# Gate matrix of an expert layer: one-hot matmuls replaced by indirect DMAs that add into HBM

## The chip, the core and the metric

The kernel runs on one core of a Trainium2 chip. The core has four compute engines that run side by side and meet through semaphores: TensorE (PE; its weight loads, PEld, are listed apart), VectorE (DVE), ScalarE (ACT) and GpSimd (POOL). SyncE (SP) here only issues DMAs. Sixteen DMA engines move data between HBM and the on-chip memory. The metric is device time of one execution in microseconds (us); less is better.

## The reference, cut to what matters

Two transformer blocks run one after the other over 256 tokens of width 1024. The first has a mixer (window attention and retention) and a gated FFN. The second has another mixer and, as its FFN, a layer of 16384 experts: each expert is one row of `expert_u` and one row of `expert_v`. Eight heads pick 16 experts each for every token, and only those 128 count, each with a softmax gate `g`:

```python
q = (xb @ w_query).reshape(PEER_TOKEN_BLOCK, PEER_HEADS, 2, PEER_HALF)
sc = jnp.einsum('thpd,hpkd->thpk', q, sub_keys).astype(jnp.float32)
s_top, i_top = lax.top_k(sc, PEER_TOPK)
cand = s_top[:, :, 0, :, None] + s_top[:, :, 1, None, :]
cand_idx = i_top[:, :, 0, :, None] * PEER_NKEYS + i_top[:, :, 1, None, :]
...
best, pos = lax.top_k(cand, PEER_TOPK)
eidx = jnp.take_along_axis(cand_idx, pos, axis=-1)
g = jax.nn.softmax(best, axis=-1)
u = jnp.take(expert_u, eidx, axis=0)
h = jax.nn.gelu(jnp.einsum('thkd,td->thk', u, xb))
vv = jnp.take(expert_v, eidx, axis=0)
return jnp.einsum('thk,thkd->td', (g * h.astype(jnp.float32)).astype(xb.dtype), vv)
```

An expert has the number 128 a + b, with a and b the picks of the head's two halves.

## The kernel before, in words

The kernel does not gather experts. It computes all 16384 of them for all tokens, in two layers. The first layer (`first_layer(j)`, j from 0 to 127) makes u x for the 128 experts of block j (all a, b = j) and puts its gelu into the matrix S (128 experts a, 128 blocks, 256 tokens) in the on-chip memory. S is multiplied by a gate matrix of the same shape, zero wherever an expert was not picked, and the second layer (`second_layer`, j from 0 to 127) sums S times v.

Every product is made in three passes for precision: a weight unit of 512 KB is loaded into a tile `raw` by SP (L89), split into a rounded part `whi` by ACT (L94) and a rest `wlo` by DVE (L95), and PE does hi x hi, hi x lo and lo x hi (`mm3`, L107 to L109). One unit of the first layer is 24 matmuls over 256 tokens. There are 433 such splits on DVE from start to end, one per unit apart from six that POOL does near the start; the first layer's last unit is the 305th, the second layer's units are the 306th to the 433rd. Four `raw` tiles and, in the expert layers, three pairs of `whi` and `wlo` let loads and splits run ahead of PE. The tile scheduler that orders each engine's instructions gives these loads and splits a higher priority (`AHEAD`), so they stand earlier than the code has them.

The picks are made beside the first queries and the first third of the first layer. For each head `choose(hd)` takes the best 16 of both halves and of 80 candidate sums on DVE. A generator (`all_steps`) yields these steps, and `pump` issues a budget of them after each query (PQ) and each first-layer unit (PU). When all eight heads are chosen, `decode()` turns the positions into pairs (a, b) with one-hot compares on DVE, makes the softmax gates, and transposes a, b and g on PE (L796) into the rows `gs`.

The gate matrix is then made four tokens at a time by `combine(jd)`, 64 times, between first-layer units: DVE makes a one-hot matrix of a (A) and of b (B), ACT and DVE scale B by the two halves of the gate (G), and PE multiplies A by G for each token and half (L872, eight matmuls of 128 x 128 per call). DVE multiplies the result into the part of S that is there already (L875), ACT writes the rest (L878), and units that come later multiply their gelu by what stands there (L934). So the end of the first layer and the gate matrix are interleaved on PE. The first block's FFN (`w_gate` and `w_up`, 22 units each) is where the change adds stores.

Of the kernel before, what the change touches and what calls it, by code (L numbers as in the profile page):

```python
# [22 lines left out]
GP = 115  # L23
# [4 lines left out]
GSCALE = 32768.0  # L28
# [7 lines left out]
for _n, _w in (("norm_mix", 8), ("norm_ffn", 8), ("final_norm", 8), ("ln_mix", 8), ("ln_ffn", 8),  # L36
               ("ret_gain", 8), ("gmlp_gain", 4), ("q_g", 1), ("k_g", 1), ("sinks", 8)):
    SMALL[_n] = (_o, _o + _w)
    _o += _w
# [3 lines left out]
class Net:  # L43
# [70 lines left out]
    def gemm_t(self, ps, src, hl, K, k0=0, first=True, last=True, parts=None, engine=None):  # L114
        """ps[n, t] += W[k, n] x[k, t] for one unit of up to 8 k."""
# [12 lines left out]
    def gemm_t_late(self, jobs, hl):  # L128
        """gemm_t of several (ps, src), with the last k after all others."""
# [6 lines left out]
    def gemm_n(self, src, hl):  # L136
        """two banks, one per 128 tokens, of [t, 512] for a chunk of 512 columns."""
# [19 lines left out]
    def rsqrt(self, y, ss, n, scale, pool=None):  # L157
        """y = (ss * scale + eps)^-1/2, all [128, n]."""
# [22 lines left out]
    def token_sums(self, acc):  # L181
        """[128 t, 2] from [128 d, 256 t] summed over d."""
# [6 lines left out]
    def rows(self, r, name):  # L189
        """[128, 256] with r of token t in column t, in every partition."""  # L190
# [40 lines left out]
    def block1(self, actp):  # L231
        nc, a, tc = self.nc, self.a, self.tc
        mult, add, sub = OP.mult, OP.add, OP.subtract
        with ExitStack():
# [125 lines left out]
            with ExitStack() as s1:  # L360
                p = self.pool("ffn", 1, s1)
                p2 = self.pool("ffn2", 2, s1)
                hid = self.new_acts(p, KF, "hid", 1)
                early = []
                for f in range(KF):
# [11 lines left out]
                    early.append((ps.rearrange("p (a t) -> p a t", a=2), None))  # L377
                    if f == 1:
                        continue
# [322 lines left out]
    def peer(self, st, x3, h, acc):  # L702
        nc, a, tc = self.nc, self.a, self.tc
        mult, add, sub = OP.mult, OP.add, OP.subtract
        with tc.using_default_side("right"):
            xb = self.new_acts(self.pool("xb", 1), tag="xb", bufs=1)
            gs = self.pool("gs", 1).tile([128, 4, T], F16, name="gs")
            qp = self.pool("query", 1)
            late = ExitStack()
            p = self.pool("topk", 1, late)  # L710
        hand = self.pool("hand", 2, st)
# [3 lines left out]
        best = p.tile([128, 8, 2, 16], F32, name="best")  # L715
        pos = p.tile([128, 8, 2, 16], U32, name="pos")
# [28 lines left out]
        def decode():  # L745
            e16 = p.tile([128, 2, 16, 8], F16, tag="cand", name="e16", bufs=2)
            t8 = p.tile([128, 8, 2, 16], U32, tag="sc", name="t8", bufs=SC)
            dec = p.tile([128, 4, 2, 16, 8], F16, tag="stop", name="dec")
            a16, b16 = dec[:, 0], dec[:, 1]

            def spot(x):
                return x.rearrange("p t k h -> p h t k")

            for e in range(2):
                yield 340, lambda: nc.vector.tensor_copy(spot(dec[:, 2 + e]), itop[:, :, :, e])
            yield 340, lambda: nc.vector.tensor_scalar(t8, pos, 56, None, op0=add)
            yield 340, lambda: nc.vector.tensor_scalar(spot(e16), pos, 72.0, 0.0, op0=sub, op1=OP.max)
            yield 340, lambda: nc.vector.tensor_scalar(t8, t8, 3, None, op0=OP.logical_shift_right)
            yield 340, lambda: nc.vector.tensor_scalar(spot(a16), t8, 8.0, 0.0, op0=sub, op1=OP.max)
            yield 340, lambda: nc.vector.tensor_scalar(t8, pos, 16.0, 8.0, op0=OP.is_lt, op1=mult)  # L760
            yield 340, lambda: nc.vector.scalar_tensor_tensor(spot(b16), spot(a16), -8.0, pos, op0=mult, op1=add)
            yield 340, lambda: nc.vector.scalar_tensor_tensor(spot(b16), t8, -8.0, spot(b16), op0=add, op1=add)
            yield 200, lambda: nc.vector.tensor_tensor(out=a16, in0=a16, in1=e16, op=add)
            yield 200, lambda: nc.vector.tensor_tensor(out=b16, in0=b16, in1=e16, op=sub)
            ex = p.tile([128, 8, 2, 16], F32, tag="itop", name="ex")
# [320 lines left out]
```

## Time and profile before

| | |
|---|---|
| three timed runs | 1341.98, 1343.14, 1346.91 us; median 1343.14 |
| profiled execution, first to last instruction (span) | 1343.6 us |
| TensorE busy | 1334.3 us, 99% |
| VectorE busy | 935.0 us, 70% |
| ScalarE busy | 768.4 us, 57% |
| GpSimd busy | 9.7 us, 1% |
| HBM read and written | 232.62 and 2.10 MB |

The profiled execution lies within the spread of the timed runs; beside its span the profile lists no other time of its own. Busy time is the share of the span in which an engine had an instruction under way; PE's instructions overlap one another, so that a matmul's own duration is longer than the step from one to the next. The chain of waits follows the work that ended last backwards, and says which engine's time makes up the span. Groups are named by source line, engine, operation and `out<-in`; buffer numbers are left out.

### The profile page before, as it was taken

Reading aid. Unit: us, or ns where it says so; the run is one execution under the profiler, and the core shown is the slowest. Engines: PE = TensorE matmul, PEld = TensorE weight load, DVE = VectorE, ACT = ScalarE, POOL = GpSimd, SP = SyncE. Lnnn points to the kernel's source line nnn. Section 1 sums busy time; section 2 is a strip of 40 time slices with the busy share of each in tenths; the row PEclk is TensorE's granted clock in tenths of the full one; section 3 lists DMA queues with packets and bytes.
Section 4 is the critical chain, followed back from the end, with each engine's and each line's share of the span. In section 5 each row is a group of like instructions: output and inputs, shape, how many; then the busy total and the mean of one; then the engine's idle time right before and its main releaser. Section 6 shows DMA issues by size and latency. Waiting matters only on the chain.

```text
span 1343.6 us, 24086 instructions
## 1 busy us (share of the span) xinstructions
PE 1334.3 (99%) x9384; PEld 1245.0 (93%) x9384; DVE 935.0 (70%) x1826; ACT 768.4 (57%) x1306; POOL 9.7 (1%) x12
## 2 busy tenths in 40 slices
PE   8999999999999999999999999999999999999998
PEld 8878999999998899999999999999998888888887
DVE  6767576766666977966996667777656666665665
ACT  5456445544455766444458887776555555555553
POOL 2000000000000000000000000000000000000000
PEclk8999999999999999999999999999999999999999
DMA  8545666666566446656564444444576666666664
GB/s 267 179 137 159 187 179 185 186 189 181 176 192 228 142 138 181 191 180 184 151 197 147 142 141 137 140 137 139 157 219 190 192 198 191 194 195 191 196 194 126
DMA packets 67633, 236.27 MB, mean 176 GB/s; under 512 B 7616, under 2 KB 9536, under 8 KB 67392
## 3 DMA queue, kind: packets, MB, share of 16 engines
q1 hardware_dynamic: 66512, 233.14, 57.1%
q8 instruction: 73, 1.20, 0.4%
q10 hardware_dynamic: 1008, 1.61, 0.3%
q14 instruction: 40, 0.33, 0.1%
HBM read 232.62 MB, written 2.10 MB: 175 GB/s over the span
## 4 chain that ended last, share of the span: by engine, by line
PE 95%; DVE 2%; DMA 1%; issue 0%; ACT 0%; POOL 0%; SPq 0%; ACTq 0%; POOLq 0%; DVEq 0%
PE ax L974 26%; PE mm L107 21%; PE mm L109 21%; PE mm L108 21%; PE ax L872 5%; DVE wlo L95 1%; DMA raw<-in_w_in_a_dram 1%; PE ax L837 0%; DMA xT<-in_xT_dram 0%; ACT whi L94 0%; PE ax L663 0%; PE ax L698 0%; PE ax L464 0%; PE ax L452 0%; PE ax L685 0%
## 5 line engine op out<-in xcount | busy, mean ns | idle before, releaser
L95 DVE TENSOR_TENSOR wlo<-raw,whi 128x1024 fp32r<-128x1024 f32 (+2 forms) x433 | 524.5, 1213 | 225.9 <-ACT whi L94 224.8
L94 ACT ACTIVATE whi<-raw 128x1024 fp32r<-128x1024 f32 (+3 forms) x439 | 458.0, 1046 | 332.9 <-PE mm L108 249.0
L107 PE MATMUL mm<-xbh,whi 128*128 128x256 f32 x1104 | 316.2, 287 | 0.0
L109 PE MATMUL mm<-xbh,wlo 128*128 128x256 f32 x1104 | 312.4, 283 | 0.8 <-DVE wlo L95 0.7
L108 PE MATMUL mm<-xbl,whi 128*128 128x256 f32 x1104 | 312.1, 283 | 0.0
L107 PE MATMUL mm<-acth,whi 128*128 128x256 f32 x848 | 241.0, 284 | 1.7 <-ACT acth L248 1.0
L108 PE MATMUL mm<-actl,whi 128*128 128x256 f32 x848 | 239.7, 283 | 0.7 <-DVE actl L249 0.7
L109 PE MATMUL mm<-acth,wlo 128*128 128x256 f32 x848 | 239.6, 283 | 0.0
L109 PEld LDWEIGHTS mm<-xbh,wlo 128*128 128x128 f32 x1104 | 210.6, 191 | 1.3 <-DVE wlo L95 1.2
L107 PEld LDWEIGHTS mm<-xbh,whi 128*128 128x128 f32 x1104 | 211.2, 191 | 0.2
L108 PEld LDWEIGHTS mm<-xbl,whi 128*128 128x128 f32 x1104 | 210.8, 191 | 0.0
L107 PEld LDWEIGHTS mm<-acth,whi 128*128 128x128 f32 x848 | 161.3, 190 | 2.8 <-ACT acth L248 1.2
L108 PEld LDWEIGHTS mm<-actl,whi 128*128 128x128 f32 x848 | 161.2, 190 | 1.6 <-DVE actl L249 1.6
L109 PEld LDWEIGHTS mm<-acth,wlo 128*128 128x128 f32 x848 | 161.3, 190 | 0.2 <-DVE wlo L95 0.2
L974 PE MATMUL ax<-wlo,keys 128*128 128x512 f32 x512 | 158.0, 389 | 0.0
L974 PE MATMUL ax<-whi,q 128*128 128x512 f32 x512 | 158.0, 389 | 0.0
L974 PE MATMUL ax<-whi,keys 128*128 128x512 f32 x512 | 157.9, 389 | 0.0
L151 ACT ACTIVATE keys<-S 128x256 fp32r<-128x256 f32 x128 | 53.4, 418 | 151.5 <-PE ax L974 151.5
L974 PEld LDWEIGHTS ax<-whi,q 128*128 128x128 f32 x512 | 96.1, 188 | 20.0
L974 PEld LDWEIGHTS ax<-wlo,keys 128*128 128x128 f32 x512 | 96.1, 188 | 19.9
L974 PEld LDWEIGHTS ax<-whi,keys 128*128 128x128 f32 x512 | 96.1, 188 | 19.8
L865 ACT ACTIVATE G<-B,ga 128x128 f16<-128x128 f16 x256 | 98.0, 575 | 0.0
(277 smaller groups left out, 1468.7 us busy)
## 6 DMA issues: line engine op xcount, KB each, us to landing
raw<-in_peer_u_dram SPq DMA_DIRECT2D x128, 512.0 KB, 3.6
raw<-in_peer_v_dram SPq DMA_DIRECT2D x128, 512.0 KB, 4.2
raw<-in_w_in_b_dram SPq DMA_DIRECT2D x32, 512.0 KB, 4.3
raw<-in_w_in_a_dram SPq DMA_DIRECT2D x31, 512.0 KB, 3.9
raw<-in_w_gate_dram SPq DMA_DIRECT2D x22, 512.0 KB, 3.6
raw<-in_w_up_dram SPq DMA_DIRECT2D x22, 512.0 KB, 3.7
raw<-in_w_out_dram SPq DMA_DIRECT2D x16, 512.0 KB, 4.3
raw<-in_w_down_dram SPq DMA_DIRECT2D x16, 512.0 KB, 3.6
```

The lines of the kernel that those rows point to most:

```text
L94: self.last_copy = nc.scalar.activation(hi[:, s], raw[:, s], AF.Copy).ins
L95: (engine or nc.vector).tensor_tensor(out=lo[:, s], in0=raw[:, s], in1=hi[:, s].bitcast(F32), op=OP.subtract)
L107: mm(ps, lhsT=left[0], rhs=right[0], start=first, stop=False)
L108: mm(ps, lhsT=left[0], rhs=right[1], start=False, stop=False)
L109: mm(ps, lhsT=left[1], rhs=right[0], start=False, stop=last)
L151: nc.scalar.activation(hi, src, AF.Copy)
L865: nc.scalar.activation(G[0][:, :, t], B[:, :, t], AF.Copy, scale=ga[:, t0 + t:t0 + t + 1])
L872: nc.tensor.matmul(C[:, t * 128:t * 128 + 128], lhsT=A[:, :, t], rhs=G[i][:, :, t], start=i == 0, stop=i == 1)
L974: nc.tensor.matmul(banks[tb][d], lhsT=s[left][:, ts], rhs=w[right][:, d * 512:d * 512 + 512], start=first, stop=end)
```

## The change

The one-hot matmuls, `combine` and the transposes are gone. Two matrices `cmat` are made in HBM, one for each half of the tokens, each 8 MB: element (a, b, t). They are zeroed by 32 stores of 512 KB that SP issues in the first block's FFN (L382). `decode` now runs four times, after every second head, for those two heads, and instead of a transposed list it makes for each pick the place 16384 a + 128 b + t in `pos` and the gate in `best`. Then `put` issues 64 indirect DMAs on POOL's queue: each takes one pick of one head for 128 tokens, and adds 128 gates of 4 bytes to 128 computed places (L809). All DMAs into one matrix are ordered by waits, each for the one before it; the two matrices are independent, which makes two chains of 128.

`gates(j)` loads four blocks j of the gate matrix from both `cmat` into a tile C (two DMAs of 256 KB on POOL's queue, three such tiles) and multiplies S by it on DVE (L937), 32 times in all. `first_layer` now always writes its whole gelu into S.

```diff
-        def combine(jd):
-            ...
-            nc.vector.tensor_tensor(out=B, in0=self.iota16, in1=spread(3), op=OP.is_equal)
-            for i in range(2):
-                if i == 0:
-                    for t in range(4):
-                        nc.scalar.activation(G[0][:, :, t], B[:, :, t], AF.Copy, scale=ga[:, t0 + t:t0 + t + 1])
-                else:
-                    nc.vector.tensor_tensor(out=G[i], in0=B, in1=spread(i), op=mult)
-            nc.vector.tensor_tensor(out=A, in0=self.iota16, in1=spread(2), op=OP.is_equal)
-            C = self.ax_bank()
-            for t in range(4):
-                for i in range(2):
-                    nc.tensor.matmul(C[:, t * 128:t * 128 + 128], lhsT=A[:, :, t], rhs=G[i][:, :, t], start=i == 0,
-                                     stop=i == 1)
-            ...
-            elif j % 2:
-                while done < T and done * (GP - start) < T * (j - start):
-                    combine(j + 1)
-        while done < T:
-            combine(128)
...
+                zero = p.tile([128, 1024], F32, name="zero")
+                nc.gpsimd.memset(zero, 0.0)
+                self.cmat = [tc.dram_tile([128 * 128 * 128, 1], F32, name=f"cmat{i}") for i in range(2)]
+                blank = [c.rearrange("(p n) o -> p (n o)", p=128) for c in self.cmat]
...
+                    for i in range(2 * f - 10, 2 * f - 8) if f >= 5 else ():
+                        if i < 32:
+                            nc.sync.dma_start(out=blank[i // 16][:, i % 16 * 1024:i % 16 * 1024 + 1024], in_=zero)
...
-        def decode():
+        def decode(h0):
...
+            for e, x in ((1, b16), (0, a16)):
+                ...
+                if e:
+                    place = p.tile([128, 64], F32, name="place")
+                    yield 130, lambda: nc.vector.scalar_tensor_tensor(
+                        place, oh[:, 0], 128.0, self.col("part").to_broadcast([128, 64]), op0=mult, op1=add)
+                else:
+                    yield 130, lambda: nc.vector.scalar_tensor_tensor(
+                        ps, spot(oh[:, 0].rearrange("p (k q) -> p k q", q=4)), 16384.0,
+                        spot(place.rearrange("p (k q) -> p k q", q=4)), op0=mult, op1=add)
...
+            def put():
+                for hd in range(2):
+                    for k in range(16):
+                        for tb in range(2):
+                            nc.gpsimd.indirect_dma_start(
+                                cmat[tb], bass.IndirectOffsetOnAxis(ap=ps[:, hd, tb, k:k + 1], axis=0),
+                                bs[:, hd, tb, k:k + 1], None, compute_op=add)
+
+            yield 10, put
...
                 yield from choose(hd)
-            yield from decode()
+                if hd % 2:
+                    yield from decode(hd - 1)
...
+            nc.scalar.activation(S[:, j - 1:j + 1], pair.rearrange("p (e t) -> p e t", e=2), AF.Gelu_apprx_tanh)
...
+        def gates(j):
+            C = cp.tile([128, 2, 4, 128], F32, name="C", bufs=3)
+            for tb in range(2):
+                nc.gpsimd.dma_start(out=C[:, tb], in_=cview[tb][:, j:j + 4])
+            Sj = S[:, j:j + 4].rearrange("p j (b t) -> p b j t", b=2)
+            nc.vector.tensor_tensor(out=Sj, in0=Sj, in1=C, op=mult)
+
+        gates(0)
+        gates(4)
...
-            if j == 32:
+            if j % 4 == 0 and j < 120:
+                gates(j + 8)
+            if j == 120:
                 groups.close()
```

The last `if` stands in the loop of the second layer; what follows it is the load of `x3`, the residual, which came at j = 32 and now comes at j = 120.

Where instructions moved, first POOL's queue. Before, POOL had nothing to do behind the two fills of the second block's mixer (L530, L532):

```order
L530 MEMSET rel_4859 64x8x64 [waits DMAHW4_49,DMAHW6_49,DVE_49,PE_49]
L532 MEMSET wsT_4862 64x8x64 [waits DMAHW5_49,Pool_49]
L1082 UNCONDITIONAL_BRANCH
```

Now the indirect DMAs follow there, the two matrices by turns. `DMASW` names the semaphore of a DMA that POOL issued: a row waits for the one two rows ahead of it.

```order
L537 MEMSET wsT_4900 64x8x64 [waits DMAHW5_49]
L809 DMA cmat0_2480<-best_5918,pos_5919 2097152x1 [waits DVE_49,PE_49,Activation_49]
L809 DMA cmat1_2481<-best_5918,pos_5919 2097152x1
L809 DMA cmat0_2480<-best_5918,pos_5919 2097152x1 [waits DMASW0_49]
L809 DMA cmat1_2481<-best_5918,pos_5919 2097152x1 [waits DMASW1_49]
L809 DMA cmat0_2480<-best_5918,pos_5919 2097152x1 [waits DMASW2_49]
L809 DMA cmat1_2481<-best_5918,pos_5919 2097152x1 [waits DMASW3_49]
```

There are 256 such rows, and behind the last of them on the same queue the 64 gate loads. The rows that wait for DVE as well are the first of each batch of 64; on DVE, the rows that release them (the write of `pos`, L796, or of `best`, L802) stand behind the 183rd, 199th, 213th and 219th wlo.

The second place is DVE at the 290th wlo, 15 units before the end of the first layer. Before, between two weight splits stood the making of one-hot tiles and the multiplies into S:

```order
L95 TENSOR_TENSOR wlo_11868<-raw_11866,whi_11867 128x1024 [waits DMAHW7_49,Activation_49]
L934 TENSOR_TENSOR S_6217<-S_6217,gt_11708 128x2x228 [waits Activation_49]
L875 SCALAR_TENSOR_TENSOR S_6217<-ax_11723,S_6217 128x110x4 [waits Activation_49]
L875 SCALAR_TENSOR_TENSOR S_6217<-ax_11745,S_6217 128x110x4 [waits PE_49]
L867 TENSOR_TENSOR G1_11846<-B_11844,gs_5868 128x512 [waits DVE_49]
L868 TENSOR_TENSOR A_11843<-iota16_139,gs_5868 128x512
L861 TENSOR_TENSOR B_11931<-iota16_139,gs_5868 128x512 [waits DVE_49,Activation_49]
L95 TENSOR_TENSOR wlo_11898<-raw_11896,whi_11897 128x1024 [waits DMAHW0_49,PE_49,Activation_49]
```

Now the first gate multiplies (L937) stand there, with the weight splits (L93 in the new numbering) between them; L150 are splits of S for the second layer:

```order
L93 TENSOR_TENSOR wlo_10782<-raw_10780,whi_10781 128x1024 [waits DMAHW7_49,PE_49,Activation_49]
L937 TENSOR_TENSOR S_6252<-S_6252,C_11275 128x2x4x128 [waits DMASW1_49,DMASW0_49]
L93 TENSOR_TENSOR wlo_10812<-raw_10810,whi_10811 128x1024 [waits DMAHW0_49,PE_49,Activation_49]
L937 TENSOR_TENSOR S_6252<-S_6252,C_11279 128x2x4x128 [waits DMASW3_49,DMASW2_49]
L150 TENSOR_TENSOR q_11294<-S_6252,keys_11293 128x256 [waits Activation_49]
L937 TENSOR_TENSOR S_6252<-S_6252,C_11309 128x2x4x128 [waits DMASW5_49,DMASW4_49]
L93 TENSOR_TENSOR wlo_10844<-raw_10842,whi_10843 128x1024 [waits DMAHW1_49,PE_49,Activation_49]
```

All 32 gate multiplies come within the next 21 weight splits, the last behind the 311th.

The third place is SP in the first block's FFN. Before, only weight loads stand there, gate and up by turns. Now the stores of zeros stand among them, some with a wait of their own:

```order
L87 DMA raw_2664<-in_w_up_dram 128x1024 [waits DMAHW2_49,DMAHW1_49,DVE_49]
L382 DMA cmat0_2480<-zero_2476 128x1024
L87 DMA raw_2714<-in_w_gate_dram 128x1024 [waits DMAHW5_49,DMAHW3_49,DVE_49]
L382 DMA cmat0_2480<-zero_2476 128x1024 [waits DMAHW4_49]
L87 DMA raw_2744<-in_w_up_dram 128x1024 [waits DMAHW7_49,DVE_49]
L87 DMA raw_2781<-in_w_gate_dram 128x1024 [waits DMAHW6_49,DMAHW0_49,DVE_49]
```

A load behind such a store is issued only after it; 32 stores stand among 37 loads.

## Rows read from the trace of the kernel before

**Rows 1.** Page, part 1: busy us, share of the span, instructions of each engine.
```profile
PE 1334.3 (99%) x9384; PEld 1245.0 (93%) x9384; DVE 935.0 (70%) x1826; ACT 768.4 (57%) x1306; POOL 9.7 (1%) x12
```

**Rows 2.** Page, part 4: the chain that ended last, by line.
```profile
PE ax L974 26%; PE mm L107 21%; PE mm L109 21%; PE mm L108 21%; PE ax L872 5%; DVE wlo L95 1%; DMA raw<-in_w_in_a_dram 1%; PE ax L837 0%; DMA xT<-in_xT_dram 0%; ACT whi L94 0%; PE ax L663 0%; PE ax L698 0%; PE ax L464 0%; PE ax L452 0%; PE ax L685 0%
```

**Rows 3.** Chain in order of time, from us 688: start, us, engine, tile, line.
```profile
688.41 0.33 PE ax L796 x3
...
712.10 1.89 PE ax L872 x16
...
955.94 0.96 PE ax L872 x8
991.45 347.52 PE ax L974 x1533
1339.00 1.37 DVE x L997 x2
```

**Rows 4.** Line L872: duration in ns (least, median, most), starts, forms.
```profile
L872 PE MATMUL ax<-G,A x512: 283/297/304, 711.9 to 956.6; 128*128 128x128 f16 x171
```

**Rows 5.** wlo on DVE from the start: stretch, length, busy (count), PEclk.
```profile
0.00:568.30 568.30, 218.72 (x183) 0.99 0.59 182
0.00:616.20 616.20, 238.25 (x199) 0.99 0.59 182
0.00:679.50 679.50, 262.56 (x219) 0.99 0.59 181
0.00:935.00 935.00, 348.36 (x290) 1.00 0.56 171
```

**Rows 6.** PE alone in the last combines and the second layer, same columns.
```profile
936.00:991.30 55.30, 55.30 (x464) 1.00 0.55 162
1000.00:1330.00 330.00, 330.00 (x1458) 1.00 0.64 192
```

**Rows 7.** DMA issues: out<-in, queue, count, KB each, median us to landing.
```profile
raw<-in_peer_v_dram SPq DMA_DIRECT2D x128, 512.0 KB, 4.2
...
out_dram<-x SPq DMA_DIRECT2D x2, 256.0 KB, 2.1
```

**Rows 8.** Page, part 5: line L95 (busy, mean ns, idle before).
```profile
L95 DVE TENSOR_TENSOR wlo<-raw,whi 128x1024 fp32r<-128x1024 f32 (+2 forms) x433 | 524.5, 1213 | 225.9 <-ACT whi L94 224.8
```

**Rows 9.** Page, part 3: all DMA queues: packets, MB, share.
```profile
q1 hardware_dynamic: 66512, 233.14, 57.1%
q8 instruction: 73, 1.20, 0.4%
q10 hardware_dynamic: 1008, 1.61, 0.3%
q14 instruction: 40, 0.33, 0.1%
```

**Rows 10.** Line L919, stores of x3t: issue ns, and us to landing.
```profile
L919 ACTq DMA_DIRECT2D x3t<-xt x4: 326/328/347, 511.7 to 516.8; - x4
...
DMA to landing us min/median/max: 2.4/3.3/6.4
```

**Rows 11.** Line L896, the loads of keys, the same.
```profile
L896 SPq DMA_DIRECT2D keys<-in_keys_dram x8: 328/342/424, 501.7 to 610.3; - x8
...
DMA to landing us min/median/max: 2.2/3.5/6.7
```

**Rows 12.** All engines in the first FFN: busy (count), PEclk, DMA, GB/s.
```profile
228.00:320.00 92.00, 92.00 (x777) 92.00 (x777) 64.88 (x95) 46.67 (x70) 0.00 (x0) 1.00 0.61 184
```

**Rows 13.** All engines near the start, the same columns.
```profile
5.00:10.00 5.00, 3.50 (x18) 2.55 (x16) 4.37 (x8) 4.26 (x12) 2.67 (x3) 0.92 1.01 323
10.00:15.00 5.00, 4.83 (x21) 4.50 (x21) 5.00 (x13) 3.02 (x8) 0.94 (x1) 0.50 0.99 379
20.00:25.00 5.00, 5.00 (x45) 5.00 (x44) 3.69 (x12) 0.36 (x2) 2.61 (x2) 1.00 0.95 304
```

More of the change, by code (lines that the diff above doesn't have):

```diff
@@ L22 @@
 QE = 3
-GP = 115
 RAWQ = 6
@@ L27 @@
 PU = 1400
-GSCALE = 32768.0
 T = 256
@@ L36 @@
 for _n, _w in (("norm_mix", 8), ("norm_ffn", 8), ("final_norm", 8), ("ln_mix", 8), ("ln_ffn", 8),
-               ("ret_gain", 8), ("gmlp_gain", 4), ("q_g", 1), ("k_g", 1), ("sinks", 8)):
+               ("ret_gain", 8), ("gmlp_gain", 4), ("q_g", 1), ("k_g", 1), ("sinks", 8), ("part", 1)):
     SMALL[_n] = (_o, _o + _w)
@@ L706, in peer @@
             xb = self.new_acts(self.pool("xb", 1), tag="xb", bufs=1)
-            gs = self.pool("gs", 1).tile([128, 4, T], F16, name="gs")
             qp = self.pool("query", 1)
+            hold = self.pool("hold", 1)
             late = ExitStack()
             p = self.pool("topk", 1, late)
+        cmat = self.cmat
+        cview = [c.rearrange("(a b t) o -> a b (t o)", a=128, b=128) for c in cmat]
         hand = self.pool("hand", 2, st)
@@ L714, in peer @@
         itop = p.tile([128, 8, 2, 2, 16], U32, name="itop")
-        best = p.tile([128, 8, 2, 16], F32, name="best")
-        pos = p.tile([128, 8, 2, 16], U32, name="pos")
+        best = hold.tile([128, 8, 2, 16], F32, name="best")
+        pos = hold.tile([128, 8, 2, 16], U32, name="pos")
         scores = {}
@@ L928, in first_layer @@
                 return
-            js = slice(j - 1, j + 1)
-            p3 = pair.rearrange("p (e t) -> p e t", e=2)
-            if done:
-                gt = cp.tile([128, 2, T], F32, name="gt", bufs=2)
-                nc.scalar.activation(gt[:, :, :done], p3[:, :, :done], AF.Gelu_apprx_tanh)
-                nc.vector.tensor_tensor(out=S[:, js, :done], in0=S[:, js, :done], in1=gt[:, :, :done], op=mult)
-            if done < T:
-                nc.scalar.activation(S[:, js, done:], p3[:, :, done:], AF.Gelu_apprx_tanh)
+            nc.scalar.activation(S[:, j - 1:j + 1], pair.rearrange("p (e t) -> p e t", e=2), AF.Gelu_apprx_tanh)
         for c in range(RAWQ):
@@ L956, in peer @@
                 if ready:
-                    start = j
                     with tc.using_default_side("right"):
                         cp = self.pool("comb", 1, groups)
-                    ga = cp.tile([128, T], F32, name="ga")
-                    nc.scalar.activation(ga, gs[:, 0], AF.Copy)
-            elif j % 2:
-                while done < T and done * (GP - start) < T * (j - start):
-                    combine(j + 1)
-        while done < T:
-            combine(128)
+        def gates(j):
[6 more added lines that the diff above has]
+        gates(4)
         banks = [[self.ax_bank() for _ in range(2)] for _ in range(2)]
@@ L1038, in layout @@
              np.tile(f["q_norm_g_2"][0], 2)[:, None], np.tile(f["k_norm_g_2"][0], 2)[:, None],
-             np.tile(f["att_sinks"][0], (128, 1))]
+             np.tile(f["att_sinks"][0], (128, 1)), np.arange(128, dtype=np.float32)[:, None]]
     out["small"] = np.concatenate(small, 1)
```

103 lines of the change are left out of this document (36 added, 67 removed).

## The prediction, made before the changed kernel was run

> **What bounds the kernel now.** I read the table of engine busy time first, then the chain of waits by line, then the same chain in order of time around the removed lines, then the pace of TensorE. TensorE (PE) is busy 1334.3 of 1343.6 us [rows 1], and the lines that end last are all PE's: the second expert layer (L974), the three-pass matmuls of all other products (L107 to L109), and the one-hot matmuls of the gate matrix (L872) with 5% [rows 2]. The reader is to see in the chain in time that PE does first-layer products and one-hot products by turns from 712.10 to 956, that the second layer starts at 991.45 and runs 347.52 us, and that 4.6 us are left behind it (1343.6 less 1338.97) [rows 3]. So a PE instruction taken away here is time taken away, as long as nothing else becomes late. The profile's span, 1343.6, lies 0.5 us above the median of the runs, 1343.14; the sum is made against the span.
>
> **What goes.** 512 one-hot matmuls: a row of the chain has 16 of them in 1.89 us [rows 3], 0.118 each; each one's own 297 ns [rows 4] overlaps the next and is not the price. 512 x 0.118 = 60.5 us. The six transposes of the old decode, three in 0.33 us [rows 3], add 0.7. Sum: 61.2 us of PE. The VectorE and ScalarE work that made the one-hot tiles goes too; it lay beside PE work, so I count it at nothing. The decode of eight heads in one piece becomes four of two heads, some 24 VectorE rows each; PE's first-layer units hide it as they hid the old one, and if that cover went it would cost at most the few us that a batch of links is released later. The first layer would now end at 991.45 - 61.2 = 930.25.
>
> **What comes, first: the chains.** 256 indirect DMAs on GpSimd's (POOL) queue, 128 into each of two matrices in HBM. Each waits until the one before it into the same matrix has landed; the two chains alternate on one queue. I call P the time of one link (a pair of DMAs, one of each chain). They come in four batches of 32 pairs. By the program's order the first batch is released by a VectorE row that stands behind the 183rd weight split (wlo), the last by one behind the 219th; the trace of before has those counts at 568.3 and 679.5, the second at 616.2 [rows 5]. The chains thus end at the latest of 568.3 + 128 P, 616.2 + 96 P and 679.5 + 32 P; for any P over 1.5 it is the first.
>
> **By when they must end.** The first gate multiply stands on VectorE behind the 290th wlo, and the 291st is queued behind it, 15 first-layer units before the second layer. PE runs a unit of 24 matmuls at 464 in 55.30 us [rows 6], 0.1192 each, 2.86 us a unit; 15 units are 42.9 us, so PE asks for wlo 291 at 930.25 - 42.9 = 887.3. Ahead of that come the gate load (512 KB; a 512 KB load of this stage lands in 4.2 us [rows 7]), the multiply and the wlo (both 128x1024 f32; such a row takes 1.21 us [rows 8]): 6.6 us. The chains must end by 880.7, which is P = (880.7 - 568.3) / 128 = 2.44 us. If they are later, VectorE stands at the multiply, PE starves for lack of weights, and the end is chain end + 6.6 + 42.9 + 347.5 + 4.6, that is 969.9 + 128 P, and no longer depends on the 61.2 us saved.
>
> **The size of P.** No row of before shows a DMA issued by POOL: the queues in the trace are hardware-generated or instruction fetch [rows 9]. Bounds: a store to HBM lands in 2.1 us where nothing else moves, at the kernel's end [rows 7]; beside the weight stream the x3t stores land in 2.4 / 3.3 / 6.4 us (least, median, most) [rows 10], the small loads (keys, 128 KB) in 2.2 / 3.5 / 6.7 [rows 11]. A link reads its destination and writes it. If the two legs overlapped wholly and nothing were added, P would be 2.1; one after the other, at their medians, 3.5 + 3.3 = 6.8. A hardware-queue issue takes 0.33 us [rows 10]; POOL's step is not shown, and two of them bound P too. I take the longer leg at its median plus one issue step, 3.5 + 0.33 = 3.8, since the chains run while weights stream at the same rate as around those rows. 128 x 3.8 = 486 us: the chains end at 1055, 174 us late.
>
> The Trainium skill, page "DMA: Bandwidth & Descriptors", section "Anatomy of one DMA — SWDGE (gpsimd) path", gives about 2.0 us fixed for a DMA issued from GpSimd, most of it the receipt of the write, longest for HBM. By that figure the links fit (an estimate: 128 x 2.0 = 256 us), and it is the first rival below. The x3t row, 3.3 us under load on the faster-issued queue, does not agree with so short a time.
>
> **Second: zeroing.** 32 stores of 512 KB on SP's queue, between the gate and up weights of the first block's FFN, 32 among some 37 loads. PE takes 37 x 24 x 0.1184 (777 in 92.00 us [rows 12]) = 105 us for those units. 69 transfers are 36.2 MB, 344 GB/s where the stage now moves 184. Two early stretches moved 323 and 379 GB/s at a DMA share of about 1 [rows 13]. So A is 0 (fits) to 36.2 MB / 323 GB/s - 105 = 7 us; what is loaded ahead covers a part; I take 3. Some of the stores wait on SP for the earlier DMA whose semaphore they take over, and the next weight loads stand behind them; the same buffers ahead cover that.
>
> **Third: gate loads and multiplies.** All 32 multiplies stand on VectorE between wlo 290 and 311, not over the whole second layer. In these 21 units (60 us of PE) VectorE has 53 rows of 1.21 us, 64 us, and the queues must bring 53 x 512 KB, 27.8 MB, 73 to 86 us at the two rates above. Seven units and three gate tiles can already lie in their buffers, 5.2 MB or some 15 us. So B is 0 (loads ahead cover it) to 26 (they cover nothing); I take 12, above the middle of what remains, since each multiply that waits holds the wlo behind it. The load of x3 (1 MB) now waits on SP for the last gate load, with weight loads behind it; their raw buffer comes free only behind the last gate multiply anyway, so I count it at nothing; uncovered it would be its 3 us of transfer at 323 GB/s.
>
> **Clock.** In the kernel's start PE had 18 matmuls in 5 us, then ran at a granted 0.50 (1.2 GHz) with 21 in 5 us, and at 1.00 with 45 [rows 13]. After a wait of 170 us I expect one such stretch: 24 matmuls of 0.119, K = 3 us; bounds 0 and 6.
>
> **Sum.** 969.9 + 486.4 + 3 + 12 + 3 = 1474 us. Made the other way: 1343.6 - 61.2 + 174 of waiting + 18 = 1474.
>
> **Rivals.** (1) *The chains fit.* P at or below 2.44, as the store at the end (2.1) and the least of the x3t stores (2.4) would have it; then nothing waits and 1343.6 - 61.2 + 3 + 12 = 1297 us (1282 to 1315 with the bounds of A and B). For it: 128 rows of 4 bytes are far less data than those stores carry. Against: no median in this stage is that short, and two DMAs go through one queue for each link. Up to P = 2.73 the time is still faster by 0.5%. (2) *A link is much slower.* The two legs follow one another (P = 6.8: 1858 us), or POOL's own step is so long that the chains do not overlap, or POOL must wait behind VectorE: one 1.21 us row ahead of each link makes 3.8 + 1.2 = 5.0 and 1628 us. For it: VectorE is 70% busy [rows 1]. Against: nothing in before shows POOL held up by VectorE. The Trainium skill, page "SBUF — State Buffer", section "SBUF: two separate sides", says that a VectorE instruction in a two-port mode keeps GpSimd from writing descriptors; no row of before can show that. (3) *The bandwidth is the bound* with chains that fit: A = 7 and B = 26, 1315 us; still faster, and part of rival 1's range. (4) *Break-even:* P = 2.73 to 2.83 puts it within 0.5%, where the wait eats what PE was spared.
>
> **Chances.** A difference of under 0.5% (7 us) is what timing can't tell from no change. Forecast, P from 2.83 to 5.05: 58%, its own range 1350 to 1630. Rival 1 with 3, P below 2.73: 22%. Break-even: 3%. Rival 2, P above 5.05: 17%. Faster 0.22, same 0.03, slower 0.75. The range for 8 in 10 takes in rival 1 and leaves out rival 2: 1290 to 1630.
>
> **What would show it.** In the profile after: no L872 rows; POOL's indirect DMAs from about 570 us on, and the spacing of one chain's issues is P; VectorE idle before the first gate multiply, released by the DMA queue; PE idle for the same stretch, ending some 400 us before the end; its granted clock low once behind the gap. Wrong if the chain's last DMA lands before 880 (then rival 1), if PE has gaps in the FFN stage of the first block of more than 7 us (then A), or if the gap is there but its length differs from 128 P (then a batch was late, or the gate loads hold PE).

## The result, and the profile after

The changed kernel takes 1575.06 us (median; 1573.71 to 1583.08) against 1342.56 (1341.73 to 1346.91) for the kernel before in the same job: a ratio of 1.174 [1.171, 1.178], slower by 233 us. The forecast was 1474 us, range 1290 to 1630: slower was right, and the time lies in the range, 101 us above the forecast.

The page of the changed kernel: busy time of each engine, then PE's share and its granted clock in 40 slices, then the chain by engine and by line, then the groups of the new lines (busy us, mean ns | idle before) and the stores of zeros among the DMA issues (KB, us to landing).

```profile
span 1571.9 us, 22787 instructions
...
PE 1279.3 (81%) x8866; PEld 1189.2 (76%) x8866; DVE 868.5 (55%) x1615; ACT 669.6 (43%) x956; POOL 506.6 (32%) x333
...
PE   8999999999999999999999500000057999999998
...
PEclk9999999999999999999999855555579999999999
...
PE 56%; POOL 21%; DMA 15%; issue 5%; DVE 2%; ACT 0%; DVEq 0%; ACTq 0%
...
L809 POOL DMA_INDIRECT cmat<-best,pos x256 | 461.7, 1804 | 266.3 <-DVE itop L731 153.0
...
L937 DVE TENSOR_TENSOR S<-S,C 128x1024 f32<-128x1024 f32 x32 | 39.1, 1223 | 291.1 <-DMA C<-cmat 290.9
...
cmat<-zero SPq DMA_DIRECT2D x32, 512.0 KB, 6.8
```

The reader is to see that PE, 99% busy before [rows 1], stands empty for six slices of 39.3 us and parts of two more, at a granted clock of 0.5 (the 1.2 GHz level), and that the chain, nearly all PE before [rows 2], now has POOL's indirect DMAs and their landings with a third of it. VectorE waits 290.9 us for gate loads, 271.7 of that before the first multiply. The end of the chain in order of time (start, us, what) answers to [rows 3]:

```profile
1143.21 1.55 POOL cmat L809
1145.06 3.06 DMA cmat<-best,pos
1148.41 3.13 DMA C<-cmat
...
1224.19 343.10 PE ax L948 x1505
```

The last indirect DMA lands at 1148.1, where the forecast had 1058 (its 1055 and the 3 of zeroing). How the chains spent the time is read from all rows of the line: durations (least, median, most), first and last start, and what ended POOL's idle time before them:

```profile
L809 POOL DMA_INDIRECT cmat<-best,pos x256: 1542/1552/2599, 571.5 to 1145.1; - x128
...
  issue: 68.6, 218
  DMA cmat<-best,pos: 44.8, 37
```

Only 37 of the 256 waited for a landing; 218 followed the one before as soon as POOL was through with it. The timeline (start, us, engine, line, idle before) shows the two paces, first beside the weight splits, then in the gap:

```profile
757.82 2.57 POOL L809 DMA_INDIRECT cmat<-best,pos  x1 [0.30 <-issue]
...
760.62 1.23 DVE L93 TENSOR_TENSOR wlo<-raw,whi 128x1024 fp32r<-128x1024 f32 x1 [1.65 <-ACT whi L92]
...
760.70 2.58 POOL L809 DMA_INDIRECT cmat<-best,pos  x1 [0.30 <-issue]
```

```profile
999.26 1.55 POOL L809 DMA_INDIRECT cmat<-best,pos  x1 [0.31 <-issue]
1001.11 1.55 POOL L809 DMA_INDIRECT cmat<-best,pos  x1 [0.30 <-issue]
```

In the gap a step, from the start of one row to the start of the next, is 1.55 + 0.30, 1.855 us on average, so a link of both chains is 3.71. Beside a weight split (wlo) the same row takes 2.58 us and a step 2.88, a link 5.76. The row that starts 0.08 us behind the start of the wlo ends 1.43 us behind its end, then come 0.30, and since the next wlo starts 1.65 us behind the last one's end, the next row is again caught by it: the two engines march in step, one indirect DMA for each weight unit.

The landing of the same DMAs (us from the start of a row, least, median, most) has two paces too, first from 680 to 886, where weights stream, then from 935 to the last:

```profile
DMA to landing us min/median/max: 3.0/5.1/6.5
...
DMA to landing us min/median/max: 2.9/3.0/3.5
```

Without the weight stream, beside the same splits, it is 4.1 (experiment 6): the stretched row makes it about 1 us longer, and the stream another 1 us.

Four stretches of all engines (PE, PEld, DVE, ACT, POOL busy (count), PEclk, DMA share, GB/s): the FFN with the zeroing, part of the gap, and the 25 us behind it.

```profile
195.00:330.00 135.00, 135.00 (x1140) 135.00 (x1140) 96.18 (x145) 69.96 (x106) 0.95 (x1) 1.00 0.90 310
...
900.00:1000.00 100.00, 0.00 (x0) 0.00 (x0) 0.00 (x0) 0.00 (x0) 83.39 (x55) 0.50 0.23 0
1150.00:1160.00 10.00, 5.95 (x28) 5.95 (x29) 7.40 (x8) 4.16 (x7) 4.28 (x9) 0.50 0.90 303
1160.00:1175.00 15.00, 12.94 (x103) 12.33 (x103) 11.96 (x12) 5.68 (x7) 6.38 (x12) 1.00 0.96 341
```

### The profile page after: what moved, and what is told of

Its sections match the earlier page's. It is cut to its first block, busy times and chain, and to the rows that moved or that the text cites. A ratio compares the mean times of both kernels' runs of the same rounds, so it can differ in the third digit from the quotient of the medians.

```text
span 1571.9 us, 22787 instructions
## 1 busy us (share of the span) xinstructions
PE 1279.3 (81%) x8866; PEld 1189.2 (76%) x8866; DVE 868.5 (55%) x1615; ACT 669.6 (43%) x956; POOL 506.6 (32%) x333
## 4 chain that ended last, share of the span: by engine, by line
PE 56%; POOL 21%; DMA 15%; issue 5%; DVE 2%; ACT 0%; DVEq 0%; ACTq 0%
PE ax L948 22%; POOL cmat L809 21%; DMA cmat<-best,pos 11%; PE mm L105 11%; PE mm L106 10%; PE mm L107 10%; DMA C<-cmat 3%; DVE S L937 1%; DVE wlo L93 1%; POOL C L935 0%; DMA small<-in_small_dram 0%; DVE actl L247 0%; PE ax L849 0%; PE ax L668 0%; PE ax L703 0%
## 5 line engine op out<-in xcount | busy, mean ns | idle before, releaser
L93 DVE TENSOR_TENSOR wlo<-raw,whi 128x1024 fp32r<-128x1024 f32 (+2 forms) x433 | 524.7, 1214 | 282.1 <-ACT whi L92 281.6
L809 POOL DMA_INDIRECT cmat<-best,pos x256 | 461.7, 1804 | 266.3 <-DVE itop L731 153.0
L107 PE MATMUL mm<-xbh,wlo 128*128 128x256 f32 x1104 | 315.7, 286 | 277.9 <-DVE wlo L93 277.9
L107 PEld LDWEIGHTS mm<-xbh,wlo 128*128 128x128 f32 x1104 | 214.1, 194 | 279.8 <-DVE wlo L93 279.8
L106 PEld LDWEIGHTS mm<-xbl,whi 128*128 128x128 f32 x1104 | 214.0, 194 | 0.0
L937 DVE TENSOR_TENSOR S<-S,C 128x1024 f32<-128x1024 f32 x32 | 39.1, 1223 | 291.1 <-DMA C<-cmat 290.9
```

The costliest lines, as they stand in the source:

```text
L93: (engine or nc.vector).tensor_tensor(out=lo[:, s], in0=raw[:, s], in1=hi[:, s].bitcast(F32), op=OP.subtract)
L106: mm(ps, lhsT=left[0], rhs=right[1], start=False, stop=False)
L107: mm(ps, lhsT=left[1], rhs=right[0], start=False, stop=last)
L809: nc.gpsimd.indirect_dma_start(cmat[tb], bass.IndirectOffsetOnAxis(ap=ps[:, hd, tb, k:k + 1], axis=0), bs[:, hd, tb, k:k + 1], None, compu ...
L937: nc.vector.tensor_tensor(out=Sj, in0=Sj, in1=C, op=mult)
```

## The experiments

My theory from this profile: POOL's own step sets the pace, not the landing (as the forecast had it), and VectorE's two-input weight splits stretch that step. Two chains hide the landing. Experiments 1 to 3, 5 to 7 and 9 test that, 10 prices the chains as a whole, and 4 and 8 try a version that is faster. All but the first contain the first one's edit; where a difference in time is told, it is against that one, 1530 us, unless another is named. Experiments 2, 3 and 5 to 7 are one run each; the four runs of the changed kernel lie 9 us apart, so the readings rest on rows of the traces and not on a few microseconds of total time.

### 1. The gate multiplies behind the last weight split

```diff
-            (engine or nc.vector).tensor_tensor(out=lo[:, s], in0=raw[:, s], in1=hi[:, s].bitcast(F32),
+            self.behind = (engine or nc.vector).tensor_tensor(out=lo[:, s], in0=raw[:, s], in1=hi[:, s].bitcast(F32),
...
-            nc.vector.tensor_tensor(out=Sj, in0=Sj, in1=C, op=mult)
+            with tc.issue_after(self.behind):
+                nc.vector.tensor_tensor(out=Sj, in0=Sj, in1=C, op=mult)
```

`issue_after` places a multiply in VectorE's order behind the weight split last issued, so the first layer can end before VectorE stands still.

> The changed kernel with one edit: every gate multiply on VectorE must stand behind the last weight split (wlo) issued in the code so far, so that none comes before wlo 305, the last of the first layer. Theory (GpSimd's own step of 1.55 us and 0.30 us between two of them makes the pace, and it is held up by VectorE's wlo rows to 2.88 us): PE runs the 15 first-layer units before the gap and not behind it (42.9 us less), the multiplies are spread over the second layer (most of the 22 us that the tail had over 401.6 go), but GpSimd is held up for 43 us longer (about 15 us later chains). Chain end about 1163, whole about 1525 us. Rival (the tail's extra 22 us come from the gate loads themselves, wherever they stand): about 1545 us.

Measured: 1530.21 us, 1.139 [1.136, 1.142] of before. Its chain in time:

```profile
1164.29 3.06 DMA cmat<-best,pos
1168.72 4.03 DMA C<-cmat
1175.26 348.81 PE ax L949 x1531
```

The tail behind the last landing falls from 423.8 us (1571.9 - 1148.1) to 361.4 (1528.7 - 1167.35), that is 62.4 less: the 42.9 of the 15 first-layer units, and 19.5 that the changed kernel lost, as I read it, because gate loads, multiplies and the held weights all came at once. In return the chains end 19.2 later: VectorE's splits go on to 930 and hold POOL at 2.88 a step for 44 us more, which is 8.4 steps or 16 us, and the rest is that two rows fewer had started by 680.

### 2. Four matrices

```diff
-                                cmat[tb], bass.IndirectOffsetOnAxis(ap=ps[:, hd, tb, k:k + 1], axis=0),
+                                cmat[tb + 2 * (k % 2)], bass.IndirectOffsetOnAxis(ap=ps[:, hd, tb, k:k + 1], axis=0),
```

The additions of odd k go into two more matrices, which nothing reads; a landing is waited for four places later.

> As the late-gates kernel, but the picks of odd k go into two further matrices that nobody reads, so that four chains of 64 replace two of 128 (the gate matrix lacks those picks; the further matrices are not zeroed). Theory (GpSimd's step sets the pace, a link's landing is covered already by the other chain): no change, within 10 us of the late-gates kernel, one DMA per 1.85 us in the quiet stretch. Rival (each link waits for the landing of the one before, so that latency sets the pace): the pace doubles, chain end near 890, whole near 1310 us.

Measured: 1511.06 us, 19 less, about twice the 10 that the theory allowed. The step beside the splits is what it was:

```profile
760.86 1.23 DVE L93 TENSOR_TENSOR wlo<-raw,whi 128x1024 fp32r<-128x1024 f32 x1 [1.66 <-ACT whi L92]
...
760.93 2.57 POOL L809 DMA_INDIRECT cmat<-best,pos  x1 [0.30 <-issue]
...
763.81 2.58 POOL L809 DMA_INDIRECT cmat<-best,pos  x1 [0.30 <-issue]
```

In the gap too it is 1.855. So from 680 on POOL is the limit and not the landing. The 19 us come from 560 to 680, where two chains did wait for landings at times (20 rows for 27.7 us in the first experiment, none here); 51 rows had started by 680 instead of 42. Some 4 of the 19 us (an estimate: two rows at 1.855) are a first batch that came 5.5 us earlier, at 568.5.

### 3. One chain

```diff
-                                cmat[tb], bass.IndirectOffsetOnAxis(ap=ps[:, hd, tb, k:k + 1], axis=0),
+                                cmat[0], bass.IndirectOffsetOnAxis(ap=ps[:, hd, tb, k:k + 1], axis=0),
```

All 256 go into one matrix, each behind the one before it (the second matrix stays zero).

> As the late-gates kernel, but all 256 indirect DMAs add into the first matrix, which makes one chain of 256 (the second half's gates stay zero, the first half's are wrong). Theory (two chains are bound by GpSimd's step, one chain by step and landing): a link takes 3.1 us to land and 0.3 to go on, about 3.4 us quiet and 4.0 beside VectorE's wlo: chain end near 1490, whole near 1850 us. Rival (the landing was the bound of two chains too, a link of 3.7 quiet and 5.0 on the way): chain end near 1720, whole near 2075 us.

Measured: 1861.32 us, as the theory said. In the gap:

```profile
1400.80 1.54 POOL L809 DMA_INDIRECT cmat<-best,pos  x1 [1.63 <-DMA cmat<-best,pos]
1403.96 1.54 POOL L809 DMA_INDIRECT cmat<-best,pos  x1 [1.62 <-DMA cmat<-best,pos]
```

Here each step does wait for the landing: in the gap a link of a single chain is 3.2 us, which is the quantity that the forecast tried to size with 3.5. Two chains cover it there (3.71 is more than 3.2), and that is why it did not decide. Beside the weights, from 680 to 920, the single chain's link was 4.6 us on average (53 links). The 5.76 of two chains held up by the splits covers that as well; 3.71 would not, which is what experiment 5 meets.

### 4. Half the tokens by indirect DMA

If POOL needs 1.86 to 2.88 us an addition and has from 568 to about 930, 126 to 195 fit (362 us by either step). So tokens 0 to 127 go through the matrices (even k into one, odd k into the other, added on VectorE after the load), and tokens 128 to 255 keep the one-hot matmuls, in 32 calls instead of 64.

```diff
+                        nc.gpsimd.indirect_dma_start(
+                            cmat[k % 2], bass.IndirectOffsetOnAxis(ap=ps[:, hd, 0, k:k + 1], axis=0),
+                            bs[:, hd, 0, k:k + 1], None, compute_op=add)
...
+            elif j % 2:
+                while done < 128 and done * (GP - start) < 128 * (j - start):
+                    combine(j + 1)
...
+            with tc.issue_after(self.behind):
+                nc.vector.tensor_tensor(out=C[:, 0], in0=C[:, 0], in1=C[:, 1], op=add)
+                nc.vector.tensor_tensor(out=Sj, in0=Sj, in1=C[:, 0], op=mult)
```

> A version meant to be used: tokens 0 to 127 by indirect DMAs (128 of them in two chains, even and odd k in a matrix each, the two added when loaded), tokens 128 to 255 by the old one-hot matmuls (32 calls, 256 matmuls, 30.4 us of PE); gate multiplies late. Theory: GpSimd needs 128 steps of 2.9 to 3.1 us beside VectorE, chain end about 955, PE ends the first layer at about 961: nothing waits, 1343.6 - 30.5 + about 5 = 1318 us. Rival (the one-hot rows on VectorE, 0.42 us each with two inputs, hold GpSimd up to 3.6 us a step): chain end near 1030, whole near 1390 us.

Measured: 1326.43 us, 0.987 [0.985, 0.989]; 1318 was expected. The last addition is issued at 879.6, in time and well before the 955 expected. Yet PE has a gap that the additions did not make (the first row is of POOL's timeline, the others of the chain that ended last):

```profile
959.64 0.60 POOL L1008 DMA_DIRECT2D C<-cmat  x1 [78.49 <-DVE S L967]
...
959.09 0.55 issue
959.64 0.59 POOL C L1008
960.23 4.39 DMA C<-cmat
964.74 0.70 DVE C L1011
...
966.66 350.39 PE ax L1023 x1533
```

The gate tiles (C) took over memory of the first layer's last tiles (gt), so the first gate load waited 78.49 us for L967, the multiply that reads gt, and so for the first layer to end.

### 5. No weight splits on VectorE beside the chains

Blocks 48 to 127 make no wlo; PE uses whi in its place.

```diff
+        if self.mode == "nolo":
+            nc.sync.dma_start(out=raw[:, :n], in_=src)
+            self.behind = nc.scalar.activation(hi, raw, AF.Copy).ins
+            return hi, hi
```

> As the late-gates kernel (1530 us), but for blocks 48 to 127 of the first layer VectorE makes no wlo; PE takes whi in its place (this leaves out the low part of those weights). All loads, PE and ScalarE work stay. Theory (VectorE's two-input row holds GpSimd's indirect DMA up, 2.88 us a step beside it): from about 697 us on a step is 1.85 us, chains end near 1086, whole near 1449 us. Rival (the traffic of the weight loads holds it up): a step stays 2.88 us until the loads end, whole near 1530 us.

Measured: 1523.17 us; the theory's 1449 was missed by 74. The row did what the theory said: 1.55 us from 700 on, so it is VectorE's split that stretches it (ScalarE's whi and the weight stream are still there). The step did not fall as far:

```profile
773.86 1.55 POOL L814 DMA_INDIRECT cmat<-best,pos  x1 [0.98 <-DMA cmat<-best,pos]
776.55 1.55 POOL L814 DMA_INDIRECT cmat<-best,pos  x1 [1.14 <-DMA cmat<-best,pos]
778.76 1.55 POOL L814 DMA_INDIRECT cmat<-best,pos  x1 [0.67 <-DMA cmat<-best,pos]
```

With POOL faster, the landing beside the weight stream is next, at 2.2 to 2.5 us a step until 880. The chains still ended at about 1120, 47 us earlier than in the first experiment. Most of that was lost by something that the edit did elsewhere:

```profile
1124.27 0.72 ACT L153 ACTIVATE keys<-S 128x256 fp32r<-128x256 f32 x2 [245.31 <-DVE S L946]
...
1125.99 0.58 PE L109 MATMUL mm<-xbh,whi 128*128 128x256 f32 x1 [239.54 <-ACT whi L86]
```

With no wlo to order them by, the splits of S stand on ACT ahead of the last first-layer weights, and 43 us of first-layer products came behind the gap (the second layer starts at 1169.23). Without that the run would have been about 1480, an estimate from these rows.

### 6. No weights loaded beside the chains

Blocks 49 to 127 of the first layer load no weights and split those of block 48 again in their place; VectorE's and POOL's work is the same.

```diff
-            nc.sync.dma_start(out=raw[:, s], in_=src[:, s])
+            if not kept:
+                nc.sync.dma_start(out=raw[:, s], in_=src[:, s])
```

> As the late-gates kernel (1530 us), but blocks 49 to 127 of the first layer load no weights: they split the tile of block 48 again and again (the product is that of block 48's weights). VectorE, ScalarE and PE work stay. Theory (VectorE): a step stays 2.88 us until the first layer ends, whole near 1530 us. Rival (weight traffic): 1.85 us from about 697 us on, whole near 1449 us.

Measured: 1530.36 us. Without the weight stream (1 GB/s from 700 to 850) the row is as long as with it, and as closely tied to the wlo:

```profile
770.25 1.23 DVE L97 TENSOR_TENSOR wlo<-raw,whi 128x1024 fp32r<-128x1024 f32 x1 [1.65 <-ACT whi L96]
...
770.32 2.58 POOL L814 DMA_INDIRECT cmat<-best,pos  x1 [0.30 <-issue]
```

So it is not DMA traffic that stretches POOL's row.

### 7. Weight splits with one input

Blocks 48 to 127 make wlo by a scaling of whi alone, a row of 0.69 us in place of 1.23.

```diff
+            nc.scalar.activation(hi, raw, AF.Copy)
+            self.behind = nc.vector.tensor_scalar(lo, hi.bitcast(F32), 2.0 ** -13, None, op0=OP.mult).ins
+            return hi, lo
```

> As the late-gates kernel (1530 us), but for blocks 48 to 127 wlo is made by a VectorE row with one input (whi times a constant; this leaves out the true low part). Theory (what holds GpSimd up is the second input of a VectorE row): a step is 1.85 us beside it, whole near 1449 us. Rival (any long VectorE row from and to the on-chip memory does): 2.4 to 2.9 us a step, whole near 1530 us; if the row itself gets shorter than 1.21 us, a step in between, near 1490 us.

Measured: 1505.21 us, nearer the middle that the expectation named than either theory. The chains ended at 1141.9.

```profile
761.98 1.55 POOL L816 DMA_INDIRECT cmat<-best,pos  x1 [1.12 <-DMA cmat<-best,pos]
...
763.61 0.69 DVE L88 TENSOR_SCALAR wlo<-whi 128x1024 fp32r<-128x1024 f32 x1 [2.18 <-ACT whi L87]
...
763.83 1.89 POOL L816 DMA_INDIRECT cmat<-best,pos  x1 [0.30 <-issue]
```

The row shown is stretched to 1.89 us, less than beside the two-input row (the mean of 40 us stretches from 680 to 920 is 1.60 to 1.73), and, as in the fifth experiment, the next limit is the landing. This row has one input and is shorter, both at once, and it still stretches POOL's row; which of the two makes the stretch smaller, the run can't tell.

### 8. Half the tokens, with memory of their own for the gate tiles

The gate tiles of the fourth experiment waited for memory. This gives the first layer's tile memory of its own (two gate tiles instead of three) and ends the one-hot calls earlier (GP 95 instead of 115):

```diff
-            gt = cp.tile([128, 2, 128], F32, name="gt", bufs=2)
+            gt = gq.tile([128, 2, 128], F32, name="gt", bufs=1)
```

> The half version again, with the 32 one-hot calls done by block 95 and the gate tiles in space that is free from then on (two of them, not three), so that the first gate loads need not wait for the end of the first layer. Theory: the gap of about 10 us at 957 to 967 us goes, 1326 - 10 = about 1316 us. Rival (faster one-hot calls hold VectorE or GpSimd up, or two gate tiles are too few): 1326 us or more.

Measured: 1312.82 us, 0.975 [0.974, 0.977] of before: faster than both kernels. Its busy time and the end of its chain:

```profile
PE 1301.3 (99%) x9125; PEld 1212.8 (92%) x9125; DVE 922.2 (70%) x1815; ACT 728.8 (56%) x1191; POOL 277.2 (21%) x205
```

```profile
960.15 347.52 PE ax L1024 x1533
```

PE has no gap. Against the tenth experiment it is 31 us longer, about the price of the 256 one-hot matmuls that are left (256 x 0.118 = 30.2).

### 9. Four matrices and one-input splits together

Experiments 5 and 7 left one question: is the landing beside the weights a limit of two chains, or of the queue itself?

```diff
-                                cmat[tb], bass.IndirectOffsetOnAxis(ap=ps[:, hd, tb, k:k + 1], axis=0),
+                                cmat[tb + 2 * (k % 2)], bass.IndirectOffsetOnAxis(ap=ps[:, hd, tb, k:k + 1], axis=0),
...
+            self.behind = nc.vector.tensor_scalar(lo, hi.bitcast(F32), 2.0 ** -13, None, op0=OP.mult).ins
```

> Four matrices as in the second experiment together with the one-input low parts of the seventh (blocks 48 to 127; the output is not the reference's, and the odd additions land in matrices that nothing reads). Theory: two separate limits were left in the two single edits. With four matrices alone the GpSimd row stays stretched to 2.575 us beside the two-input rows (pitch 2.88); with one-input rows alone the row falls to 1.6 to 1.73 us, but each addition then waits for the landing of the one two places before it (pitch 2.2 to 2.9 from 680 to 920). Together neither is left: pitch 1.9 to 2.05 us from 680 to 920 (98 additions there before, about 120 now, 22 more by 1.855 = 41 us), and 560 to 680 gains the 19 us that four matrices gave. Chain end 1141.9 - 41 - 19 = 1082, time 1505 - 60 = 1445 us (1430 to 1465). Rival: the landing of an indirect addition beside streaming weights is limited by the queue itself, whatever it waits for; then only the 19 us come, 1486 us (1476 to 1496).

Measured: 1439.57 us, 1.072 [1.068, 1.076]; the theory's 1445.

```profile
762.23 1.55 POOL L816 DMA_INDIRECT cmat<-best,pos  x1 [0.30 <-issue]
...
762.69 0.69 DVE L88 TENSOR_SCALAR wlo<-whi 128x1024 fp32r<-128x1024 f32 x1 [2.18 <-ACT whi L87]
...
764.08 1.55 POOL L816 DMA_INDIRECT cmat<-best,pos  x1 [0.30 <-issue]
765.94 1.74 POOL L816 DMA_INDIRECT cmat<-best,pos  x1 [0.30 <-issue]
```

No row waits for a landing now, and the step is 1.92 us on average from 760 to 920. The landing beside the weights was thus a limit of two chains and not, at this pace, of the queue. The single edits gained 19 and 25 us, both together 91: each alone had met the other limit.

### 10. No indirect DMAs

The first experiment without the 256 additions: the matrices stay zero, and so does what the second layer sums. Zeroing, gate loads and multiplies stay.

```diff
-            yield 10, put
```

> The first experiment (gates multiplied late) without the 256 indirect additions: the matrices stay zero, so the second layer's activations are zero too; zeroing, gate loads and multiplies stay. Theory: all that the change adds apart from the chains is nearly free once no chain is waited for: first layer ends at 932 as in the first experiment, the second layer follows at once with 347.5 to 349 us on PE and 4.6 us behind it: 1286 us (1280 to 1295), which is 244 us below the first experiment, and that is the price of the chains. Rival: the 64 gate loads and 32 two-input multiplies disturb the second layer even when nothing waits for a chain (the tail of the changed kernel was 22 us longer than its parts): 1300 to 1315 us.

Measured: 1281.95 us, 0.955 [0.951, 0.958].

```profile
926.42 347.52 PE ax L948 x1533
```

Next to the first experiment the chains cost 248 us. All else that the change brings shows no cost in this run: the second layer's 347.52 us is what it was in [rows 3], and starts 65.0 us earlier (991.45 - 926.42).

## Why the prediction was right, and what in it was not

**What bounds, what goes.** Right. Without the chains the second layer starts at 926.42; the forecast had 930.25.

**The deadline and the formula of the late case.** Right. In the changed kernel PE's first layer stopped at about 886.6 (forecast: wlo 291 asked for at 887.3), and VectorE stood at the first multiply, with the 291st wlo behind it, for 271.7 us. The end no longer depended on the 61 us saved.

**Batches.** Right. The first batch set the start, at 571.5 instead of 568.3; no later batch was waited for.

**The size of P: the step that failed.** The forecast took 3.8 us from the landing of hardware-queue stores plus one issue, for chains that run beside streaming weights throughout. The average was 576.6 / 128 = 4.50 (571.5 to 1148.1), and it was not one pace but two. By the forecast's own reading PE stands still from 887, and from there to the end of the chains no weights streamed (0 GB/s in the gap). In that gap a landing took 3.0 us and a single chain's link 3.2, less than the 3.5 assumed; the term that it named and didn't size, "POOL's step", was the larger: two steps of 1.855 are 3.71. That alone would have ended the chains at 1048 (571.5, 255 steps and the last landing), within 10 us of the forecast's 1058. So 3.8 was near for the quiet stretch by luck, by another mechanism than it argued.

The other 100 us were lost while weights streamed: 44 steps from 571.5 on took 110 us instead of 82, for waits on slow landings and stretched rows, and 73 steps from 680 to 886 took 206 instead of 135, held by VectorE's splits. Landing was also slower there than the forecast's 3.5 (5.1 us median, a single chain's link 4.6), but mostly hidden behind POOL's step; with that step freed it came forth (experiment 5: the chains end 47 us earlier, not 81 as its theory had it), and four matrices and one-input rows together moved their end by 89 us, to about 1078 (experiment 9).

**Rival 2** named this mechanism, POOL held by one 1.21 us row in each link, and put it at P = 5.0 and above, at 17%, because nothing in the trace of before showed POOL held up. Nothing could, as POOL had 12 instructions in all there [rows 1]. It held POOL in every step and not once a link (P = 5.76), but only while weights streamed, so the average came out below 5.05. The Trainium skill, page "SBUF — State Buffer", section "SBUF: two separate sides", has VectorE and GpSimd share a port pair as an exclusive lock, which a VectorE instruction takes also with two inputs in SBUF, against a GpSimd instruction that reads SBUF. The indirect rows agree: 2.58 us beside the two-input split, 1.55 without it, and the traffic makes no difference (experiments 5 and 6). The prediction had quoted only the part on two-port modes. Yet one-input rows held POOL too, up to 2.01 us (experiment 7), so that the second input is what decides is not shown. The plain gate loads on the same queue took 0.536 us (median) and 0.599 at most even beside two-input rows, so not every DMA issue is held.

**Rival 1** did not come about: neither the landing (a single chain's link of 3.2 us at best, experiment 3) nor POOL's step (1.855 with four matrices too, experiment 2) lets a link take 2.44. The 2.0 us of the Trainium skill's page "DMA: Bandwidth & Descriptors", section "Anatomy of one DMA — SWDGE (gpsimd) path", which it could lean on, was too short for an accumulating indirect DMA to HBM here: the least landing was 2.9 us. With 2.0 it would still not have fitted, as POOL's step alone gives 3.71.

**Zeroing, A.** Forecast 3 (0 to 7), measured nothing: 1140 matmuls from 195 to 330, at 310 GB/s and a DMA share of 0.90, against 1141 in the same stretch before:

```profile
195.00:330.00 135.00, 135.00 (x1141) 135.00 (x1140) 96.18 (x146) 70.24 (x106) 0.00 (x0) 1.00 0.62 185
```

The stores landed in 6.8 us, and PE, busy throughout, did not wait for them.

**Gate loads and clock, B + K.** Forecast 12 + 3, measured 423.8 - 401.6 = 22. The granted clock was 0.50 in the first 10 us behind the gap, with 28 matmuls in 5.95 us: 0.21 each instead of 0.119, so K was about 2.6, near the 3. B, the rest, was larger than the 12: the queues moved 303 to 341 GB/s at a share of 0.90 to 0.96, as argued for loads as the bound, and the first experiment, which spreads the multiplies, recovered 19.5 of the 22.

**The sum.** Chains 1148.1 instead of 1057.7 (+90.4), tail 7 longer than the forecast's (22 for 15): 1474 + 97 = 1571, the profiled span. Nine tenths of the miss are the size of P.

**What stays open.** Why a row is held for 1.03 us and not for the whole wlo, and what POOL does in its 1.55 us, is not shown by any run. That the two engines meet at a shared port is argued, not shown; the runs show that VectorE's row is the cause, and no run changed the number of its inputs and left its length as it was. That the plain loads escape because they read nothing of SBUF on POOL is argued, not tested. I didn't try more than half of the tokens by indirect DMA.

## What to carry to other kernels

Before moving work to an engine that has been idle, size its own step, times the count of instructions, against the time it has: here 256 steps of at least 1.855 us were 475 us in a window of 312, and no number of chains could mend that. Look also for what its new neighbours do to it: a trace in which one of two engines is idle can't show how they hold each other up. And size a wait for the traffic of the stretch in which it falls: here the landing had one length beside the weights and another in the gap. A change that replaces all of something may win when it replaces the half that fits: half of the tokens gave 0.975, all of them 1.174.

## What the hardware showed that I had not expected

- An indirect DMA of 128 elements of 4 bytes that adds to HBM costs GpSimd 1.55 us and 0.30 before the next, whatever the chains; it lands 3.0 us (median) after issue in the gap and 5.1 beside weight stream and splits. A plain 256 KB load on the same queue costs it 0.536 us.
- A two-input VectorE row of 1.23 us stretches it to 2.57, and the two engines lock in phase at the period of the weight units, 2.88 us. A one-input row of 0.69 us stretches it less: 1.74 and 1.89 us in the rows shown, 2.01 at most.
- Two limits in series hide each other: taking away one gained 19 or 25 us, both 91.
- 32 stores of 512 KB beside the weight loads raised the traffic from 185 to 310 GB/s without costing PE a matmul that could be seen.
